# Three of six k-tile pairs of the last down projection by seven block products, and its last bank in two parts

## The chip, the cores and the metric

The kernel runs on one core of a Trainium2 chip. A core has a matrix engine (TensorE, PE in the profile; PEld is its weight load), a vector engine (VectorE, DVE), a scalar engine (ScalarE, ACT), a general engine (GpSimd, POOL) and a queue engine (SyncE, SP) that here only issues transfers. The metric is the device time in microseconds (us) of one execution; less is better.

## The reference

The reference is one block of a diffusion transformer: modulated normalisation, a projection, a gated recurrence and windowed attention side by side, a merge, and a feed-forward part with a depthwise convolution. The change lies in the last product of the feed-forward part alone.

```python
def conv_ffn(h, w_up, conv_w, conv_b, w_down):
    a, u = jnp.split(h @ w_up, 2, axis=-1)
    return (jax.nn.silu(depthwise_conv(a, conv_w, conv_b)) * u) @ w_down
...
        ffn_x = conv_ffn(modulate(x_mid, norm2_g[l], mod_x[:, 3], mod_x[:, 4]), w_up[l], conv_w[l], conv_b[l], w_down[l])
        new_x = x_mid + mod_x[:, 5][:, None, :] * ffn_x
```

There are 256 tokens and 2048 columns; the inner width is 5632, which is 44 tiles of 128 rows of `w_down` (k-tiles). All is in 32-bit floats.

## The kernel before

**Numbers in two parts.** TensorE works on a rounded 32-bit format here, so each operand is split into a high part and a low rest: ScalarE casts the raw tile to `whi`, and VectorE subtracts it from the raw tile to give `wlo` (`chunk`, lines 149 and 150, or `split`, lines 159 and 160). A product then takes three matmuls, high by high, high by low and low by high (`mm3`, line 72). Weights come from the array `wst` in the order of use, in tiles of 128 x 1024 (512 KB) into five raw buffers, by SP's queue; `whi` and `wlo` have three buffers each.

**The feed-forward part.** The 44 inner tiles are made in three groups of 16, 16 and 12 (`FF_GROUPS`). `up(g, gt)` makes a group: for each tile `duo` runs 16 steps of four matmuls into two banks, and `up_evac` folds these, applies the convolution and the gate, and splits the result into `gt`. After two groups, `down_two` adds up the first 32 k-tiles of the down projection; then the third group is made, and `down` adds up the last 12 k-tiles, multiplies by the gate (`gate`), adds to the rows kept in `xn`, and writes `out`. The down projection has 256 tokens (two halves of 128, the matmul's stationary side) by 2048 columns, which are taken as two halves of 1024 (`n`), each of two blocks of 512 (`c`). So a k-tile gives four products of 128 x 128 by 128 x 512 in each half, into four banks.

**Seven products.** `half` (lines 968 to 1030), used by `down_two` alone, takes k-tiles in pairs, so that the two token halves by the two tiles form a 2 x 2 block matrix, and the two tiles by the two column blocks another. For the pairs in `SEVEN`, the eight block products are replaced by seven, in the Winograd form of Strassen's rule. It needs sums of activation blocks, made once in `seven_acts` when the up tiles are evacuated, and sums of weight blocks, made in each half by VectorE from the raw tiles (`four`, lines 1011 to 1014) and then cast and split like any weight (`r2`, `r4`). Three products go straight into the `norm` banks of the plain pairs, and four into banks of their own (`sev`). After the last of the seven pairs VectorE joins the `sev` banks into `y` (lines 1023 to 1027), which is added to the `norm` banks at the end (line 1030). PSUM has eight banks: five in the pool `mm` (`bankm` in the profile) and three in `ms` (`banks`).

**The last down projection before.** `down` (lines 1053 to 1071) uses plain products: 12 k-tiles in each half, the last two taken bank by bank, so that the four banks close one after the other. For each bank VectorE multiplies by the gate (line 1067) and adds to `xn` (line 1068), and SP issues the output (line 1071).

**What sets the order.** A planner places the instructions: each engine's queue is fixed beforehand, by priority among those that the planner thinks ready. Program order is the priority. `tc.high_priority(offset)` moves work ahead: weight chunks by up to `LEAD` = 60 instructions, ends of a stage by `RUSH` = 120, and work at `-LAG` is put back by 60. Within `chunk`, `issue_after` keeps the casts and the splits in the order of the stream. Small tasks (`tasks`) are taken one at each `tick`, of which `duo` has four per up tile. SP's queue holds the loads and the outputs, and an issue waits there for its buffer with all others behind it.

Of the kernel before, what the change touches and what calls it, by code (L numbers as in the profile page):

```python
# [33 lines left out]
          ("m64", T)]  # L34
FF_GROUPS = [(0, 16), (16, 16), (32, 12)]
SEVEN = (1, 3, 5, 7, 9, 11, 13)


def offsets(fields):
# [12 lines left out]
def block_kernel(ctx, tc, xct, prm, cst, ada2, wst, out):  # L52
# [105 lines left out]
    def split(hi, lo, src):  # L158
        S.copy(hi, src)
        V.tensor_tensor(lo, src, hi.bitcast(F32), op=ALU.subtract)  # L160

    def exp_silu(dst, src, tmp):
        S.activation(tmp, src, AF.Exp, scale=-1.0)
# [761 lines left out]
    def up_evac(g, gt, i, oa, ou, fold=fold):  # L925
        f = FF_GROUPS[g][0] + i
        t, s = fs1[:, f % 4, :], fs2[:, f % 4, :]
        fold(s, oa)
        S.activation(t, s, AF.Identity, bias=cb[:, f:f + 1], scale=cw[:, f, 1:2])  # L929
        V.scalar_tensor_tensor(t[:, 1:T], s[:, 0:T - 1], cw[:, f, 0:1], t[:, 1:T], op0=ALU.mult, op1=ALU.add)  # L930
        V.scalar_tensor_tensor(t[:, 0:T - 1], s[:, 1:T], cw[:, f, 2:3], t[:, 0:T - 1], op0=ALU.mult, op1=ALU.add)
        fold(s, ou)
        S.activation(t, t, AF.Silu)
        V.tensor_tensor(s, s, t, op=ALU.mult)
# [13 lines left out]
    def seven_acts(p, gt, i, s1, s2):  # L948
        if not sums:
            sums["b"] = big.tile([P, 2, 2, 3 * P], F32R, name="sb", tag="sb")  # L950
        n = SEVEN.index(p)
        if n == 2:
            sums["a"] = big.tile([P, 5, 2, 3 * P], F32R, name="sa", tag="qo")
        d = sums["b"][:, n] if n < 2 else sums["a"][:, n - 2]
        sums[p] = d
        w = scr.tile([P, 512], F32, name="t")
        V.tensor_tensor(w[:, 0:P], s1[:, P:], s2[:, P:], op=ALU.subtract)
# [7 lines left out]
        for i in range(i0, FF_GROUPS[g][1]):  # L965
            up_evac(g, gt, i, *duo((h2, h2)))

    def half(g0, g1, norm, sev, y, own):
# [5 lines left out]
        def add(b, a, w, start=False, stop=False):  # L974
            mm3(b, *a, *w, start, stop)
        first = SEVEN[0]
        for p in range(16):
            k1, k2 = 2 * p, 2 * p + 1
            rb, (w21, w22) = chunk(2, fetch)
            a11, a21, a12, a22 = act(k1, 0), act(k1, 1), act(k2, 0), act(k2, 1)  # L980
            if p not in SEVEN:
                st0, sp = p == 0, p == 15
                if sp:
                    ra, (w11, w12) = chunk(2, fetch)
                    for b, u1, u2, v1, v2 in ((0, a11, a12, w11, w21), (1, a11, a12, w12, w22), (2, a21, a22, w11, w21),
                                              (3, a21, a22, w12, w22)):
                        add(norm[b], u1, v1)
                        add(norm[b], u2, v2, stop=True)
                    break
                add(norm[0], a12, w21, st0)  # L990
                add(norm[2], a22, w21, st0)
                add(norm[1], a12, w22, st0)
                add(norm[3], a22, w22, st0)
                ra, (w11, w12) = chunk(2, fetch)
                add(norm[0], a11, w11)
                add(norm[2], a21, w11)
                add(norm[1], a11, w12)
                add(norm[3], a21, w12)
                continue
            f, l = p == first, p == SEVEN[-1]  # L1000
            d = sums[p]
            s1, s2, s4 = [(d[:, 0, i * P:i * P + P], d[:, 1, i * P:i * P + P]) for i in range(3)]
            add(norm[0], a12, w21)
            add(norm[1], s4, w22)
            ra, (w11,) = chunk(1, fetch, home=own)
            add(sev[0], a11, w11, f, l)

            r4 = strm.tile([P, 1024], F32, name="araw", bufs=2)

            def four(raw):  # L1010
                V.tensor_tensor(raw[:, 0:512], ra[:, 0:512], ra[:, 512:], op=ALU.add)
                V.tensor_tensor(raw[:, 512:], ra[:, 512:], rb[:, 512:], op=ALU.add)  # L1012
                V.tensor_tensor(r4[:, 0:512], raw[:, 0:512], rb[:, 512:], op=ALU.add)
                V.tensor_tensor(r4[:, 512:], r4[:, 0:512], rb[:, 0:512], op=ALU.add)
            r2, (t1, t3) = chunk(2, four, "araw")
            add(sev[1], s1, t1, f, l)
            add(sev[3], a21, t3, f, l)

            _, (t2, t4) = chunk(2, lambda raw: None, r4)
            add(sev[2], s2, t2, f, l)  # L1020
            add(norm[2], a22, t4)
            if l:
                S.copy(y[0], sev[0])
                V.tensor_tensor(y[2], sev[2], y[0], op=ALU.subtract)
                V.tensor_tensor(y[1], sev[1], y[2], op=ALU.add)
                V.tensor_tensor(y[2], sev[3], y[2], op=ALU.add)
                V.tensor_tensor(y[3], sev[3], y[1], op=ALU.add)
        with tc.high_priority(offset=RUSH):
            for b in range(4):
                V.tensor_tensor(y[b], norm[b], y[b], op=ALU.subtract if b == 2 else ALU.add)  # L1030

    def down_two(g0, g1):
        own = big.tile([P, 2, 512], F32R, name="wone", tag="acc")
        own = [own[:, i] for i in range(2)]
# [4 lines left out]
        half(g0, g1, norm, sev, y0, own)  # L1039
# [4 lines left out]
        half(g0, g1, norm, sev, y1, own)  # L1044
        return y0, y1

    def gated(n, b, y):
        c = slice(512 * (b % 2), 512 * (b % 2) + 512)
        r = xn[:, b // 2, n, c]
        V.tensor_tensor(y, y, gate[n][:, c], op=ALU.mult)  # L1050
        V.tensor_tensor(r, r, y, op=ALU.add)

    def down(gt, nk):
        for n in range(2):
            norm = [bank() for _ in range(4)] if not n else [bank()] + [bank(ms) for _ in range(3)]
            w = {}
            for k in range(nk):
                ra, w[k] = chunk(2, fetch)
                ks = (k,) if k < nk - 2 else () if k < nk - 1 else (k - 1, k)
                for c, tt in ((0, 0), (0, 1), (1, 0), (1, 1)):  # L1060
                    for q in ks:
                        ts = slice(tt * P, tt * P + P)
                        mm3(norm[2 * c + tt], gt[:, q, 1, ts], gt[:, q, 0, ts], *w[q][c], q == 0, q == nk - 1)
            for c, tt in ((0, 0), (0, 1), (1, 0), (1, 1)):
                cs = slice(512 * c, 512 * c + 512)
                m = scr.tile([P, 512], F32, name="t")
                V.tensor_tensor(m, norm[2 * c + tt], gate[n][:, cs], op=ALU.mult)
                V.tensor_tensor(xn[:, tt, n, cs], xn[:, tt, n, cs], m, op=ALU.add)
                if n or tt:
                    o = slice(tt, tt + 1) if n else slice(0, 2)  # L1070
                    nc.sync.dma_start(out[:, o, n, cs], xn[:, o, n, cs])

    for i in range(2):
        up_evac(0, g0, i, os[2 * i], os[2 * i + 1], fold_pre)
# [30 lines left out]
    tasks += [lambda b=b: gated(0, b, y0[b]) for b in range(4)]  # L1105
    fs1 = big.tile([P, 4, T], F32, name="fs1", tag="kT")
    fs2 = big.tile([P, 4, T], F32, name="fs2", tag="va")
    up(2, g0)
    down(g0, FF_GROUPS[2][1])


_INS = ["xct", "prm", "cst", "ada2", "wst"]
# [147 lines left out]
```

## Time and profile before

| what | us |
|---|---|
| median of three runs (1665.59 to 1666.55) | 1665.6 |
| the profiled execution | 1666.65 |
| its span, first to last instruction | 1664.9 |
| TensorE busy in the span | 1648.2 |
| DVE busy in the span | 1241.8 |
| ACT busy in the span | 838.2 |

The span is the time between the first and the last instruction that the profile holds; what the execution has beyond it (1.75 us) lies around it. Busy time of TensorE is pipelined: matmuls overlap, and their ends are modelled, so the distance between starts is the better measure of their cost.

### The profile page before, as it was taken

Reading aid. Unit: us, or ns where it says so; the run is one execution under the profiler, and the core shown is the slowest. Engines: PE = TensorE matmul, PEld = TensorE weight load, DVE = VectorE, ACT = ScalarE, POOL = GpSimd, SP = SyncE. Lnnn points to the kernel's source line nnn. Section 1 sums busy time; section 2 is a strip of 40 time slices with the busy share of each in tenths; the row PEclk is TensorE's granted clock in tenths of the full one; section 3 lists DMA queues with packets and bytes.
Section 4 is the critical chain, followed back from the end, with each engine's and each line's share of the span. In section 5 each row is a group of like instructions: output and inputs, shape, how many; then the busy total and the mean of one; then the engine's idle time right before and its main releaser. Section 6 shows DMA issues by size and latency. Waiting matters only on the chain.

```text
span 1664.9 us, 23855 instructions
## 1 busy us (share of the span) xinstructions
PE 1648.2 (99%) x8981; PEld 1369.6 (82%) x8981; DVE 1241.8 (75%) x1914; ACT 838.2 (50%) x1267; POOL 68.1 (4%) x132
## 2 busy tenths in 40 slices
PE   8999999999999999999999999999999999999998
PEld 4668888888888888888888988888888888888887
DVE  3448986666879876768769887788776888986655
ACT  4336543444645654444445665555555555545542
POOL 0000100000000000001100000000000000000000
PEclk9999999999999999999999999999999999999999
DMA  9996834534466666977856567577555665655554
GB/s 379 407 372 233 301 114 156 189 114 152 165 214 210 223 213 227 335 238 277 286 203 232 186 216 266 200 278 263 192 180 187 202 214 197 222 196 190 187 189 148
DMA packets 104723, 372.83 MB, mean 224 GB/s; under 512 B 11536, under 2 KB 13728, under 8 KB 104608
## 3 DMA queue, kind: packets, MB, share of 16 engines
q1 hardware_dynamic: 86176, 304.20, 51.8%
q0 software_dynamic: 18432, 67.12, 12.4%
q8 instruction: 70, 1.15, 0.3%
q14 instruction: 45, 0.37, 0.1%
HBM read 369.16 MB, written 2.11 MB: 223 GB/s over the span
## 4 chain that ended last, share of the span: by engine, by line
PE 89%; DVE 4%; issue 3%; DMA 2%; ACT 1%; POOL 0%; SPq 0%; DVEq 0%; ACTq 0%; POOLq 0%
PE bankm L70 78%; PE banks L70 9%; DVE wlo L116 1%; DMA ringv<-in_wst_dram 1%; DMA ringkT<-in_wst_dram 1%; DVE acc L407 1%; PE banks L782 0%; PE banks L415 0%; DMA araw<-in_ada_dram 0%; DMA ringq<-in_wst_dram 0%; PE banks L615 0%; PE banks L810 0%; PE banks L607 0%; DMA xraw<-in_xct_dram 0%; PE banks L1080 0%
## 5 line engine op out<-in xcount | busy, mean ns | idle before, releaser
L116 DVE TENSOR_TENSOR wlo<-raw,whi 128x1024 fp32r<-128x1024 f32 (+2 forms) x410 | 499.0, 1218 | 228.7 <-ACT whi L115 225.5
L115 ACT CAST whi<-raw 128x1024 fp32r<-128x1024 f32 (+2 forms) x410 | 428.3, 1045 | 459.0 <-PE bankm L70 411.7
L70 PE MATMUL bankm<-hl,whi 128*128 128x512 f32 (+1 forms) x2048 | 627.7, 389 | 0.1
L70 PE MATMUL bankm<-whi,hl 128*128 128x512 f32 x1640 | 526.4, 393 | 1.0 <-ACT hl L252 0.9
L70 PE MATMUL bankm<-hl,wlo 128*128 128x256 f32 (+2 forms) x1760 | 396.6, 293 | 1.5 <-DVE wlo L116 1.5
L70 PEld LDWEIGHTS bankm<-hl,wlo 128*128 128x128 f32 x1760 | 330.8, 188 | 75.6 <-DVE wlo L116 2.4
L70 PEld LDWEIGHTS bankm<-whi,hl 128*128 128x128 f32 x1640 | 307.4, 188 | 66.1 <-ACT hl L252 2.6
L70 PEld LDWEIGHTS bankm<-hl,whi 128*128 128x128 f32 x2048 | 327.8, 189 | 17.8 <-DVE fs L916 0.4
L70 PE MATMUL bankm<-wlo,hl 128*128 128x512 f32 x820 | 320.3, 391 | 0.0
L70 PEld LDWEIGHTS bankm<-wlo,hl 128*128 128x128 f32 x820 | 154.1, 188 | 31.2 <-DVE wlo L116 0.2
L407 DVE SCALAR_TENSOR_TENSOR acc<-araw,csil,acc 128x1024 f32<-128x1024 f32 x120 | 153.5, 1279 | 2.1 <-DMA araw<-in_ada_dram 1.7
L150 DVE TENSOR_TENSOR wlo<-raw,whi 128x1024 fp32r<-128x1024 f32 x74 | 90.2, 1224 | 41.2 <-ACT whi L149 38.9
L402 POOL DMA_DIRECT2D araw<-in_ada_dram x128 | 67.9, 531 | 1091.4 <-DVE acc L407 569.3
L149 ACT CAST whi<-raw 128x1024 fp32r<-128x1024 f32 x74 | 77.7, 1053 | 66.4 <-PE bankm L70 41.1
L70 PE MATMUL bankm<-yb,whi 128*128 128x512 f32 x256 | 80.9, 397 | 0.0
L70 PEld LDWEIGHTS bankm<-yb,wlo 128*128 128x128 f32 x256 | 48.1, 188 | 11.2
L929 ACT ACTIVATE fs<-fs,prm 128x256 f32<-128x256 f32 x44 | 26.4, 601 | 52.0 <-DVE fs L464 52.0
L70 PE MATMUL bankm<-yb,wlo 128*128 128x256 f32 x256 | 50.6, 279 | 0.0
L149 ACT CAST whi<-araw 128x1024 fp32r<-128x1024 f32 x28 | 29.4, 1052 | 39.0 <-DVE araw L1012 34.9
L70 PE MATMUL banks<-whi,hl 128*128 128x512 f32 x136 | 46.3, 389 | 0.0
L70 PE MATMUL bankm<-whi,g 128*128 128x512 f32 x124 | 41.3, 390 | 0.0
L70 PEld LDWEIGHTS bankm<-yb,whi 128*128 128x128 f32 x256 | 39.2, 189 | 0.1
(291 smaller groups left out, 1523.3 us busy)
## 6 DMA issues: line engine op xcount, KB each, us to landing
raw<-in_wst_dram SPq DMA_DIRECT2D x489, 512.0 KB, 4.1
araw<-in_ada_dram POOLq DMA_DIRECT2D x128, 512.0 KB, 4.7
ringv<-in_wst_dram SPq DMA_DIRECT2D x24, 512.0 KB, 10.0
ringq<-in_wst_dram SPq DMA_DIRECT2D x20, 512.0 KB, 9.9
araw<-in_wst_dram SPq DMA_DIRECT2D x10, 512.0 KB, 9.9
xraw<-in_xct_dram SPq DMA_DIRECT2D x8, 512.0 KB, 6.9
raw<-in_wst_dram SPq DMA_DIRECT2D x7, 384.0 KB, 9.9
ringkT<-in_wst_dram SPq DMA_DIRECT2D x5, 512.0 KB, 9.9
```

The source lines that it names most:

```text
L70: return PE.matmul(o, l, r, start=start, stop=stop, skip_group_check=True)
L115: S.copy(hi, raw)
L116: self.last = V.tensor_tensor(lo, raw, hi.bitcast(F32), op=ALU.subtract)
L149: a = S.copy(hi[:, w], raw[:, w])
L150: b = V.tensor_tensor(lo[:, w], raw[:, w], hi[:, w].bitcast(F32), op=ALU.subtract)
L402: nc.gpsimd.dma_start(raw, ada2[idx])
L407: V.scalar_tensor_tensor(acc, raw, csil[:, kt, 0:1], acc, op0=ALU.mult, op1=ALU.add)
L929: S.activation(t, s, AF.Identity, bias=cb[:, f:f + 1], scale=cw[:, f, 1:2])
```

## The change

A second tuple, `LATE`, names pairs 17, 19 and 20 of the whole down projection, which are pairs 1, 3 and 4 of the six pairs of the last 12 k-tiles. `up_evac` and `seven_acts` make the activation sums for them too, in homes that are free by then. `half` becomes general and is used by `down` as well; the order of the two tiles of a pair in the weight stream is swapped accordingly.

For the first half (`n` = 0) the sums of weights are made on the spot, as in `down_two`. For the second half, three tasks (`make`) run during the up tiles of the third group: each loads the two raw tiles of its pair, makes the four sums on VectorE and splits them into `pm` or `pq`; `half` then takes them from `made`. The raw tiles of these pairs are loaded again in the second half, for the products that need no sums.

In the first half the joined `y` is added to the banks, then multiplied by the gate and added to `xn` (`gated`, put back by `LAG`), then written. In the second half `combine` calls `post` after the join: it multiplies each `y` by the gate and adds it to `xn`; at the end each `norm` bank is multiplied by the gate into `y`, added to `xn` and written. The last bank (`tail`) is summed, multiplied, added and written in two parts of 256 columns.

```diff
+LATE = (17, 19, 20)
...
+    def combine(sev, y, post):
+        S.copy(y[0], sev[0])
+        V.tensor_tensor(y[2], sev[2], y[0], op=ALU.subtract)
+        V.tensor_tensor(y[1], sev[1], y[2], op=ALU.add)
+        V.tensor_tensor(y[2], sev[3], y[2], op=ALU.add)
+        V.tensor_tensor(y[3], sev[3], y[1], op=ALU.add)
+        if post:
+            for b in range(4):
+                post(b)
...
+                        for w in [slice(0, 512)] if not tail or b < 3 else [slice(0, 256), slice(256, 512)]:
+                            add(norm[b][:, w], u1, [v[:, w] for v in v1])
+                            add(norm[b][:, w], u2, [v[:, w] for v in v2], stop=True)
...
+            s1, s2, s4, *s3 = sums[p]
+            add(norm[0], a12, w21, st0)
+            add(norm[1], s4, w22, st0)
+            ra, (w11,) = chunk(1, fetch, home=own)
+            add(sev[0], a11, w11, f, l)
+            if p in made:
+                t1, t3, t2, t4 = made[p]
+                add(sev[1], s1, t1, f, l)
+                add(sev[3], s3[0] if s3 else a21, t3, f, l)
+                add(sev[2], s2, t2, f, l)
+                add(norm[2], a22, t4, st0)
+                if l:
+                    combine(sev, y, post)
+                continue
...
-        if g < 2 and f // 2 in SEVEN:
+        if f // 2 in SEVEN + LATE:
...
+            if not n:
+                half(act, 6, seven, sums_of, (norm, lambda: sev), y, own)
+                with tc.high_priority(offset=-LAG):
+                    for b in (0, 2, 1, 3):
+                        gated(0, b, y[b])
+                        if b > 1:
+                            cs = slice(512 * (b % 2), 512 * (b % 2) + 512)
+                            nc.sync.dma_start(out[:, :, 0, cs], xn[:, :, 0, cs])
+                continue
+            half(act, 6, seven, sums_of, (norm, lambda: sev), y, own, made, lambda b: gated(1, b, y[b], ALU.subtract if b == 2 else ALU.add), True)
+            with tc.high_priority(offset=RUSH):
+                for b in range(4):
+                    tt, c = b // 2, b % 2
+                    for w in [slice(0, 512)] if b < 3 else [slice(0, 256), slice(256, 512)]:
+                        cs = slice(512 * c + w.start, 512 * c + w.stop)
+                        V.tensor_tensor(y[b][:, w], norm[b][:, w], gate[1][:, cs], op=ALU.mult)
+                        V.tensor_tensor(xn[:, tt, 1, cs], xn[:, tt, 1, cs], y[b][:, w], op=ALU.add)
+                        nc.sync.dma_start(out[:, tt, 1, cs], xn[:, tt, 1, cs])
...
+    def make(p, home):
+        rb, ra = [strm.tile([P, 1024], F32, name="raw", bufs=5) for _ in range(2)]
+        for i, r in enumerate((rb, ra)):
+            nc.sync.dma_start(r, wst[wst.shape[0] - 12 + 2 * p + i])
+        r2, r4 = [strm.tile([P, 1024], F32, name="araw", bufs=2) for _ in range(2)]
+        V.tensor_tensor(r2[:, 0:512], ra[:, 0:512], ra[:, 512:], op=ALU.add)
+        V.tensor_tensor(r2[:, 512:], ra[:, 512:], rb[:, 512:], op=ALU.add)
+        V.tensor_tensor(r4[:, 0:512], r2[:, 0:512], rb[:, 512:], op=ALU.add)
+        V.tensor_tensor(r4[:, 512:], r4[:, 0:512], rb[:, 0:512], op=ALU.add)
+        for i, r in enumerate((r2, r4)):
+            split(home[:, i, 0], home[:, i, 1], r)
+        made[p] = [(home[:, i, 0, c:c + 512], home[:, i, 1, c:c + 512]) for i in range(2) for c in (0, 512)]
+    for p, home in zip((1, 3, 4), (pm[:, 0], pm[:, 1], pq)):
+        tasks += [lambda: None] * 9 + [lambda p=p, home=home: make(p, home)]
     up(2, g0)
-    down(g0, FF_GROUPS[2][1])
+    assert not tasks
+    down(g0, made)
```

More of the change, by code (lines that the diff above doesn't have):

```diff
@@ L160, in split, with half, add, four @@
         V.tensor_tensor(lo, src, hi.bitcast(F32), op=ALU.subtract)
+    def combine(sev, y, post):
[7 more added lines that the diff above has]
+                post(b)
+    def half(act, n, seven, sums, banks, y, own, made={}, post=None, tail=False):
+        norm, sev = banks
+        def add(b, a, w, start=False, stop=False):
+            mm3(b, *a, *w, start, stop)
+        for p in range(n):
+            k1, k2 = 2 * p, 2 * p + 1
+            rb, (w21, w22) = chunk(2, fetch)
+            a11, a21, a12, a22 = act(k1, 0), act(k1, 1), act(k2, 0), act(k2, 1)
+            st0 = p == 0
+            plain = p == min(set(range(n)) - set(seven))
+            if p not in seven:
+                if p == n - 1:
+                    ra, (w11, w12) = chunk(2, fetch)
+                    for b, u1, u2, v1, v2 in ((0, a11, a12, w11, w21), (1, a11, a12, w12, w22), (2, a21, a22, w11, w21),
+                                              (3, a21, a22, w12, w22)):
+                        for w in [slice(0, 512)] if not tail or b < 3 else [slice(0, 256), slice(256, 512)]:
+                            add(norm[b][:, w], u1, [v[:, w] for v in v1])
+                            add(norm[b][:, w], u2, [v[:, w] for v in v2], stop=True)
+                    break
+                add(norm[0], a12, w21, st0)
+                add(norm[2], a22, w21, st0)
+                add(norm[1], a12, w22, st0)
+                add(norm[3], a22, w22, plain)
+                ra, (w11, w12) = chunk(2, fetch)
+                add(norm[0], a11, w11)
+                add(norm[2], a21, w11)
+                add(norm[1], a11, w12)
+                add(norm[3], a21, w12)
+                continue
+            f, l = p == seven[0], p == seven[-1]
+            if f:
+                sev = sev()
+            s1, s2, s4, *s3 = sums[p]
+            add(norm[0], a12, w21, st0)
+            add(norm[1], s4, w22, st0)
[10 more added lines that the diff above has]
+                continue
+            r4 = strm.tile([P, 1024], F32, name="araw", bufs=2)
+            def four(raw):
+                V.tensor_tensor(raw[:, 0:512], ra[:, 0:512], ra[:, 512:], op=ALU.add)
+                V.tensor_tensor(raw[:, 512:], ra[:, 512:], rb[:, 512:], op=ALU.add)
+                V.tensor_tensor(r4[:, 0:512], raw[:, 0:512], rb[:, 512:], op=ALU.add)
+                V.tensor_tensor(r4[:, 512:], r4[:, 0:512], rb[:, 0:512], op=ALU.add)
+            r2, (t1, t3) = chunk(2, four, "araw")
+            add(sev[1], s1, t1, f, l)
+            add(sev[3], s3[0] if s3 else a21, t3, f, l)
+            _, (t2, t4) = chunk(2, lambda raw: None, r4)
+            add(sev[2], s2, t2, f, l)
+            add(norm[2], a22, t4, st0)
+            if l:
+                combine(sev, y, post)
+        if post:
+            return
+        with tc.high_priority(offset=RUSH):
+            for b in range(4):
+                V.tensor_tensor(y[b], norm[b], y[b], op=ALU.subtract if b == 2 else ALU.add)
@@ L162, in exp_silu, with parts_of @@
+    def parts_of(hi, lo):
+        return [(hi[:, i:i + P], lo[:, i:i + P]) for i in range(0, hi.shape[-1], P)]
     def exp_silu(dst, src, tmp):
@@ L950, in seven_acts @@
             sums["b"] = big.tile([P, 2, 2, 3 * P], F32R, name="sb", tag="sb")
[L951 removed]
+        n = (SEVEN + LATE).index(p)
         if n == 2:
             sums["a"] = big.tile([P, 5, 2, 3 * P], F32R, name="sa", tag="qo")
[L954 removed]
+        d = sums["b"][:, n % 7] if n % 7 < 2 else spare2 if n > 7 else sums["a"][:, n - 2]
         sums[p] = d
@@ L966, in up, with down_two @@
             up_evac(g, gt, i, *duo((h2, h2)))
-    def half(g0, g1, norm, sev, y, own):
+    def down_two(g0, g1):
+        own = big.tile([P, 2, 512], F32R, name="wone", tag="acc")
+        own = [own[:, i] for i in range(2)]
         def act(k, tt):
@@ L972, in act @@
             return gt[:, k % 16, 1, ts], gt[:, k % 16, 0, ts]
[L974 to L1034, printed above, removed]
+        sums_of = {p: parts_of(sums[p][:, 0], sums[p][:, 1]) for p in SEVEN}
         sev = [bank()]
@@ L1038, in down_two @@
         y0 = [scr.tile([P, 512], F32, name="t") for _ in range(3)] + [scr.tile([P, 512], F32, name="rs", bufs=1)]
-        half(g0, g1, norm, sev, y0, own)
+        half(act, 16, SEVEN, sums_of, (norm, lambda: sev), y0, own)
         norm = [bank()] + [bank(ms) for _ in range(3)]
@@ L1043, in down_two, with gated @@
         y1 = [y1[b // 2][:, b % 2] for b in range(4)]
-        half(g0, g1, norm, sev, y1, own)
+        half(act, 16, SEVEN, sums_of, (norm, lambda: sev), y1, own)
         return y0, y1
-    def gated(n, b, y):
+    def gated(n, b, y, op=ALU.add):
         c = slice(512 * (b % 2), 512 * (b % 2) + 512)
@@ L1050, in gated @@
         V.tensor_tensor(y, y, gate[n][:, c], op=ALU.mult)
-        V.tensor_tensor(r, r, y, op=ALU.add)
-    def down(gt, nk):
-        for n in range(2):
[L1055 to L1071, printed above, removed]
@@ new lines, in gated, with down, act @@
+        V.tensor_tensor(r, r, y, op=op)
+    def down(gt, made):
+        def act(k, tt):
+            ts = slice(tt * P, tt * P + P)
+            return gt[:, k, 1, ts], gt[:, k, 0, ts]
+        sums_of = {p - 16: parts_of(sums[p][:, 0], sums[p][:, 1]) for p in LATE}
+        seven = tuple(sums_of)
+        own = [own2[:, i] for i in range(2)]
+        for n in range(2):
+            if n:
+                norm = [bank()] + [bank(ms) for _ in range(3)]
+                sev = [bank() for _ in range(4)]
+                y = [big.tile([P, 2, 512], F32, name="y" + t, tag=t) for t in ("kT", "va")]
+                y = [y[b // 2][:, b % 2] for b in range(4)]
+            else:
+                sev = [bank()]
+                norm = [bank() for _ in range(4)]
+                sev += [bank(ms) for _ in range(3)]
+                y = [scr.tile([P, 512], F32, name="t") for _ in range(3)] + [scr.tile([P, 512], F32, name="rs", bufs=1)]
+            if not n:
[6 more added lines that the diff above has]
+                            nc.sync.dma_start(out[:, :, 0, cs], xn[:, :, 0, cs])
+                continue
+            half(act, 6, seven, sums_of, (norm, lambda: sev), y, own, made, lambda b: gated(1, b, y[b], ALU.subtract if b == 2 else ALU.add), True)
+            with tc.high_priority(offset=RUSH):
+                for b in range(4):
+                    tt, c = b // 2, b % 2
[4 more added lines that the diff above has]
+                        nc.sync.dma_start(out[:, tt, 1, cs], xn[:, tt, 1, cs])
```

9 lines of the change are left out of this document (8 added, 1 removed).

## The prediction

> **What bounds the kernel now.** I read four views in this order: the page's busy shares, the table of stretches, the timeline of VectorE and of TensorE around the last down projection, and the DMA issues. First the page, then the table of stretches (first half of the big down projection, the last 12 up tiles, the last down projection up to its last matmul; the columns are the busy time of each engine, the granted clock and the DMA).
>
> ```profile
> span 1664.9 us, 23855 instructions
> PE 1648.2 (99%) x8981; PEld 1369.6 (82%) x8981; DVE 1241.8 (75%) x1914; ACT 838.2 (50%) x1267; POOL 68.1 (4%) x132
> ...
> core 0: us, PE busy (x) PEld busy (x) DVE busy (x) ACT busy (x) POOL busy (x), PEclk, DMA share, GB/s
> 1297.00:1379.20 82.20, 81.95 (x360) 66.91 (x359) 73.41 (x88) 45.06 (x50) 0.00 (x0) 1.00 0.62 205
> ...
> 1461.00:1594.40 133.40, 133.40 (x768) 116.48 (x767) 92.87 (x128) 69.87 (x104) 0.00 (x0) 1.00 0.55 190
> 1594.40:1660.00 65.60, 65.60 (x290) 53.89 (x288) 37.84 (x42) 24.92 (x27) 0.00 (x0) 1.00 0.50 167
> ```
>
> TensorE is busy 99% at the full clock (1.00 in each stretch), and in the last two stretches it never pauses: 133.40 of 133.40 and 65.60 of 65.60 us. DVE has room: 92.87 of 133.4 us in the up tiles, 37.84 of 65.6 in the last down projection. In the big down projection, which already uses the seven-product pairs, DVE stands at 73.41 of 82.2 in the half where it makes the weight sums.
>
> The end is told by three timelines: TensorE's first and last matmul of the last down projection, two pieces of the chain of waits, and DVE's last eight operations (start, length, engine, line).
>
> ```profile
> 1594.44 0.40 PE L70 MATMUL bankm<-whi,hl 128*128 128x512 f32 x1
> 1659.62 0.39 PE L70 MATMUL banks<-whi,hl 128*128 128x512 f32 x1
> ```
> ```profile
> 1628.05 2.04 PE banks L70 x9
> 1630.09 0.68 PE bankm L70 x3
> ```
> ```profile
> 1655.97 0.69 DVE L1067 TENSOR_TENSOR t<-bankm,cst 128x512 f32<-128x512 f32 x1 [1.77 <-PE bankm L70]
> 1656.69 0.69 DVE L1068 TENSOR_TENSOR xn<-xn,t 128x512 f32<-128x512 f32 x1
> 1657.33 0.69 DVE L1067 TENSOR_TENSOR t<-banks,cst 128x512 f32<-128x512 f32 x1
> ...
> 1660.05 0.69 DVE L1067 TENSOR_TENSOR t<-banks,cst 128x512 f32<-128x512 f32 x1
> 1660.77 0.69 DVE L1068 TENSOR_TENSOR xn<-xn,t 128x512 f32<-128x512 f32 x1
> ```
>
> One matmul of 512 columns costs (2.04 + 0.68) / 12 = **0.2267 us** of TensorE's time; its 0.39 us is length, overlapped with the next. There are 12 tiles x 2 halves x 4 products x 3 = 288 of them. 287 x 0.2267 = 65.06 us after 1594.44 is 1659.50, and the row says 1659.62, so only 0.12 us was lost. DVE follows at 1.36 us per bank (1655.97 to 1657.33), exactly the pace of TensorE (6 x 0.2267), so one bank's two operations stick out: DVE ends at 1660.77 + 0.69 = 1661.46, and the output's landing and the end marker take the 3.44 us to 1664.9.
>
> **The change part by part.**
>
> Products. Three pairs of six lose one of eight products in each half: 3 x 2 x 3 = 18 matmuls, 18 x 0.2267 = 4.08 us of TensorE. The two-part end puts 12 matmuls of 256 columns for 6 of 512, some tenths more; it matters only where TensorE sets the end, which the next part denies.
>
> Behind the products. The seven-product form ends with sums. After the last seven pair DVE runs four operations to join the `sev` banks, and in the second half `post` adds eight more (multiply by the gate and add to `xn`, for four banks), all of 512 columns. The join's first operation reads `sev[2]`, the last of the four `sev` banks to close, and everything else follows from it; even the gate product of `y[0]` has to wait until the join has read `y[0]`. Then each `norm` bank takes its multiply and add, which overwrite `y[b]` and so stand behind `post(b)`. That makes 12 + 6 operations of 512 columns and 4 of 256 on DVE after `sev[2]`. The seven pairs are 1, 3 and 4 of 0 to 5, so behind `sev[2]` TensorE has just 3 + 24 matmuls: 27 x 0.2267 = 6.1 us. The pace of such operations, from the gates after the big down projection, and of 256-column ones from the up tiles:
>
> ```profile
> 1463.76 0.68 DVE L1050 TENSOR_TENSOR ykT<-ykT,cst 128x512 f32<-128x512 f32 x1
> 1464.37 0.68 DVE L1050 TENSOR_TENSOR yva<-yva,cst 128x512 f32<-128x512 f32 x1
> ...
> 1585.54 0.42 DVE L464 TENSOR_TENSOR fs<-bankm,fs 128x256 f32<-128x256 f32 x1
> 1589.22 0.43 DVE L934 TENSOR_TENSOR fs<-fs,fs 128x256 f32<-128x256 f32 x1
> ```
>
> Independent ones start 0.61 us apart, one that needs its predecessor 0.72 (1655.97 to 1656.69). The 12: 12 x 0.61 = 7.3 at least, 12 x 0.665 = 8.0 if every second waits; I take the middle, 7.6. The three full banks: 3 x 1.36 = 4.1. The four halves at 0.42 to 0.43: 1.6. Together **13.3 us** (13.7 with 8.0, and 12.6 if no operation on a full bank waits either: 7.3 + 6 x 0.61 + 1.6), twice the 6.1 us of matmuls beside it. So the end moves from TensorE to DVE, and the removed products of the last pair are worth nothing there.
>
> Where `sev[2]` closes. Up to it TensorE runs 288 - 18 - 27 = 243 matmuls. Without a stall the last one starts at 1594.44 + 242 x 0.2267 = 1649.30 and ends at 1649.69. Two stalls come on top, both in the first half, where DVE makes the weight sums on the spot. The big down projection shows the work of one seven pair and one plain pair on DVE, with TensorE's use of the first sums:
>
> ```profile
> 1316.42 2.58 DVE L150 TENSOR_TENSOR wlo<-raw,whi 128x1024 fp32r<-128x1024 f32 x2 [0.59 <-ACT whi L149]
> 1318.92 0.68 DVE L150 TENSOR_TENSOR wone<-raw,wone 128x512 fp32r<-128x512 f32 x1
> ...
> 1321.45 0.69 DVE L1014 TENSOR_TENSOR araw<-araw,raw 128x512 f32<-128x512 f32 x1
> 1322.06 2.50 DVE L150 TENSOR_TENSOR wlo<-araw,whi 128x1024 fp32r<-128x1024 f32 x2
> 1324.62 1.23 DVE L150 TENSOR_TENSOR wlo<-raw,whi 128x1024 fp32r<-128x1024 f32 x1
> ```
> ```profile
> 1324.20 0.39 PE L70 MATMUL banks<-wlo,sa 128*128 128x512 f32 x1
> ```
>
> A seven pair takes DVE 1.25 (its first tile, half of the 2.50 from 1316.42 to 1318.92) + 5.70 (1318.92 to 1324.62) = 6.95 us, where TensorE needs 21 x 0.2267 = 4.76. A plain pair takes the other 1.25 and 1.2 for the tile at 1324.62, 2.45 against 24 x 0.2267 = 5.44. Alternating, 9.4 stands against 10.2 and DVE keeps up; the low part of the first sums was ready at 1322.06 + 1.23 = 1323.29 and wanted at 1324.20 (the first matmul with `wlo` in the banks of the small pool), a margin of 0.91 us. Pairs 3 and 4 of the new order are both seven pairs. Between their first sums DVE needs 6.95, TensorE 4.76: short by 2.19, less the margin is **1.3 us** of stall. Pair 5, the last, uses both its tiles at once. DVE makes the low part of the second sums, of tile one and of tile two after that, 3 x 1.2 = 3.6 us, and TensorE has 12 matmuls = 2.72 until it wants the last of these: **0.9 us**. (Slots don't help: three `whi`/`wlo` buffers hold one and a half pairs.) In the second half the sums are ready beforehand, so a seven pair costs DVE only 1.85 us, and nothing stalls.
>
> The other stall is at the start. The first seven pair meets the evacuation of the last up tile on DVE and in the banks, as it did in the big projection, where TensorE's starts lie too far apart:
>
> ```profile
> 1301.76 0.39 PE L70 MATMUL bankm<-whi,sb 128*128 128x512 f32 x1
> 1302.19 0.50 PE L70 MATMUL banks<-whi,sb 128*128 128x512 f32 x1
> 1302.53 0.40 PE L70 MATMUL banks<-whi,hl 128*128 128x512 f32 x1
> 1303.14 0.50 PE L70 MATMUL banks<-whi,sb 128*128 128x512 f32 x1 [0.21 <-ACT whi L149]
> 1303.47 0.40 PE L70 MATMUL bankm<-whi,hl 128*128 128x512 f32 x1
> ```
>
> Four starts with 0.43, 0.34, 0.61 and 0.33 us before the next instead of 0.23 are 0.8 us lost. The bank count is the same (one `sev`, four `norm`, all five of `mm`), so I take **0.7** over the 0.12 lost now, with 0 and 1.5 as bounds. The sum of the stalls is 0.8 + 1.3 + 0.9 = 3.0 (0 if the planner's order and buffers cover all, 5 if the join's operations also slip between the tiles of pair 5).
>
> Work moved into the up tiles. Three times DVE makes the sums of weights: four operations of 0.68 and two splits of 1.22 = 5.2 us, with two loads of 512 KB on SP's queue and two raw slots of five; the activation sums come on top, of whose operations these are two rows:
>
> ```profile
> L957 DVE TENSOR_TENSOR t<-fs x7: 284/286/293, 989.3 to 1256.7; 128x128 f32<-128x128 f32 x7
> L160 DVE TENSOR_TENSOR sa<-t,sa 128x384 fp32r<-128x384 f32 x3 | 1.7, 555 | 0.4 <-ACT sa L159 0.4
> ```
>
> Four of 0.286 and a split of 0.555 after one of about 0.28, less 0.14 for the shorter split of the even tile, give 1.8. In all 3 x (5.2 + 1.8) = 21 us, so DVE goes from 92.87 to 114 of 133.4 us, 85%. The big projection ran at 73.41 of 82.2 (89%) with a loss of 0.25 us, so I cost it at **0.2 us**; the cover is DVE's idle 3.4 us per up tile ((133.4 - 92.87) / 12) and the three buffered tiles. Without cover each block of 5.2 overruns one tile's idle by 1.8, 5.4 us in all. Behind a make's two loads on SP the stream's loads queue, and ScalarE's casts wait for these; the stretch moves 190 GB/s at a DMA share of 0.55, and 6 loads of 512 KB in 133.4 us add 24 GB/s, so I add nothing. In the first half's end the two outputs wait on SP for `gated` as they did for the old multiply and add, and the second half's loads queue behind them; there were as many DVE operations before them as now less the join, and DVE has 30 us there for some 21 us of work, so this too is 0 (2 if a load came late by one output's wait).
>
> The last output. Its size falls from 256 to 128 KB.
>
> ```profile
> out_dram<-xn SPq DMA_DIRECT2D x2, 512.0 KB, 4.2
> out_dram<-xn SPq DMA_DIRECT2D x4, 256.0 KB, 2.0
> ```
>
> By these rows, 4.2 us for 512 KB and 2.0 for 256, proportion would give 1.0 less; if the time doesn't shrink, 0. I take the middle, 0.5. The Trainium skill ("DMA: Bandwidth & Descriptors", section "Anatomy of one DMA") speaks against proportion: a transfer on GpSimd's path has a fixed part of about 2 us, mostly the receipt of the write, and only the rest goes with the bytes. By that rule the gain would be 0.3 (an estimate, 128 KB at the page's 436 GB/s) and the sum 0.2 higher; the rows, on SP's path, do not bear the fixed part out, since half the bytes took half the time, though the larger two ran beside the stream.
>
> The sum. `sev[2]` closes at 1649.69 + 3.0 + 0.2 = 1652.9; 0.05 for the signal and 13.3 later DVE ends at 1666.2. Before it was 1661.46: +4.8, less 0.5 for the output is **+4.3 us**. Against the profiled execution's own 1666.65 (its span and 1.75 around it) that is 1670.9; the median of the three runs lies 1.05 lower at 1665.6, so I predict **1669.9 us**.
>
> **The rivals.**
>
> A, no stall in the first half at pairs 3 to 5. For it: the planner may let DVE run ahead during the plain pairs, and 0.59 us of idle per period stood there. Against: that idle was a wait on a buffer, not on work. The stalls of 1.3 and 0.9 go: 1667.7.
>
> B, the up tiles stall too. For it: 21 us more on DVE and two of five raw slots lent out. Against: the 89% above. At half of the 5.4 it gives 1672.6.
>
> C, the other side, not slower: TensorE still sets the end. The mechanism is that the planner pulls the products of pair 4 in the second half ahead, since their sums are made early and wait for no streamed tile, so that the join and `post` run beside the matmuls. For it: TensorE is 99% busy and DVE is not. It decides once `sev[2]` closes 4.3 us, 19 matmuls, before where I put it (then as before), and at 6 us earlier TensorE sets the end alone: 1665.6 - 4.08 = 1661.5 without stalls, 1664.5 with all 3.0. Against: the join starts from `sev[0]`, which needs pair 4's streamed second tile. The Trainium skill ("Perfetto Trace Analysis", section "Identifying the Most-Contended Engine") would have it so: the engine with the highest occupancy is the one to optimise first. The page of the profile bears that out for the whole span, at 99%; whether it holds for the last 15 us is what this rival asks.
>
> D, the two-part end does not do what it says. It shortens the wait behind the last bank only if DVE is waiting for that bank. With DVE 7 us behind, the four short operations cost 1.6 us for 1.36; this 0.2 is in the forecast, and C is the only case where the split helps.
>
> **How the numbers follow.** Forecast 0.51, A 0.24, B 0.17, C 0.08; D is no case of its own. A measurement of this kernel tells about 0.2%, 3.3 us, from no change: below 1662.3 is faster, above 1668.9 slower. The forecast's own range is 1668 to 1672 (chain 12.6 to 13.7, stalls 2 to 4), nine tenths of it above the line: 0.46. With B 0.17 and 0.04 of A that makes 0.67 slower. C is faster only where the stalls stay away too, 0.04. The rest, 0.05 of the forecast, 0.20 of A and 0.04 of C, is 0.29 for the same. The range reaches from A with the shortest chain and the quickest output, 1667.7 - 0.7 - 0.5 = 1666.5, and a little of C, 1665.8, to a little beyond B, 1673.0.
>
> **What would show it.** Right: in the second half DVE runs some 22 operations without a gap after the last read of `sev[2]`, TensorE's last matmul ends about 7 us before DVE's last operation, and the chain of waits ends in DVE for 13 us, not 5.5. TensorE shows pauses of about 1 us in pair 4 and at pair 5 of the first half and none in the second; the up stretch stays at 133.4 to 133.6 us. Wrong: TensorE's last matmul within 2 us of DVE's end (C), an up stretch longer by over 1 us (B), or a first half of 135 x 0.2267 = 30.6 us without pauses (A).

## The result and the profile after

The changed kernel takes 1669.53 us (median of 15 runs, 1667.71 to 1670.41) against 1665.59 us before (median of 15, 1664.64 to 1666.57): 3.9 us more, a ratio of 1.0020 with a 95% interval of 1.0014 to 1.0027. The forecast was 1669.9.

The page of the changed kernel, and its row of the table of stretches for the 12 up tiles; behind it the row of the kernel before, cut at the same two matmuls. The columns are the stretch and its length, then the busy time of PE, PEld, DVE, ACT and POOL, the granted clock and the DMA.

```profile
span 1666.2 us, 23950 instructions
PE 1645.8 (99%) x8969; PEld 1365.7 (82%) x8969; DVE 1280.9 (77%) x1990; ACT 849.9 (51%) x1287; POOL 68.1 (4%) x132
...
1458.94:1592.69 133.75, 133.75 (x770) 116.71 (x768) 110.09 (x165) 77.76 (x116) 0.00 (x0) 1.00 0.62 213
```
```profile
1460.69:1594.44 133.75, 133.75 (x770) 116.79 (x768) 93.11 (x129) 70.18 (x104) 0.00 (x0) 1.00 0.55 190
```

TensorE is busy for 2.4 us less in all (the rest of the 4.08 us of removed matmuls is taken by short pauses, most of which busy time counts as work), and VectorE for 39 us more. The up tiles take 133.75 us in both kernels, with VectorE at 110.09 in place of 93.11: the sums made there cost no time.

The last down projection begins at 1592.69 us. These rows are TensorE's first and last matmul in it.

```profile
1592.69 0.40 PE L71 MATMUL bankm<-whi,hl 128*128 128x512 f32 x1
...
1656.84 0.28 PE L71 MATMUL banks<-whi,hl 128*128 128x256 f32 x1
```

And this is VectorE behind `sev[2]` in the second half (line 165 reads it; 165 to 168 are the join, 1076 and 1077 the gate operations of `post`, 1112 and 1113 those of the `norm` banks):

```profile
1651.04 0.69 DVE L165 TENSOR_TENSOR yva<-bankm,ykT 128x512 f32<-128x512 f32 x1 [2.90 <-PE bankm L71]
1651.77 0.69 DVE L166 TENSOR_TENSOR ykT<-bankm,yva 128x512 f32<-128x512 f32 x1
1652.38 0.68 DVE L1076 TENSOR_TENSOR ykT<-ykT,cst 128x512 f32<-128x512 f32 x1
...
1657.17 0.69 DVE L1112 TENSOR_TENSOR ykT<-banks,cst 128x512 f32<-128x512 f32 x1
1657.77 0.69 DVE L1076 TENSOR_TENSOR yva<-yva,cst 128x512 f32<-128x512 f32 x1
...
1661.97 0.76 DVE L1112 TENSOR_TENSOR yva<-banks,cst 128x256 f32<-128x256 f32 x2
1662.64 0.76 DVE L1113 TENSOR_TENSOR xn<-xn,yva 128x256 f32<-128x256 f32 x2
```

TensorE is done at 1656.84 + 0.28 = 1657.12. VectorE works without a gap of over 0.03 us from 1651.04 to 1662.64 + 0.76 = 1663.40, 22 operations in 12.36 us, of which the last 6.28 us stand alone. Before, 1.46 us stood alone.

TensorE's pauses lie in the first half. Below are its rows at pair 1 and at pairs 4 and 5; starts of neighbours should be 0.23 us apart.

```profile
1599.53 0.39 PE L71 MATMUL bankm<-whi,sb 128*128 128x512 f32 x1
1599.96 0.50 PE L71 MATMUL banks<-whi,sb 128*128 128x512 f32 x1
1600.30 0.40 PE L71 MATMUL banks<-whi,hl 128*128 128x512 f32 x1
1600.90 0.50 PE L71 MATMUL banks<-whi,sb 128*128 128x512 f32 x1 [0.21 <-ACT whi L150]
...
1616.43 0.73 PE L71 MATMUL banks<-whi,hl 128*128 128x512 f32 x2
1617.73 0.50 PE L71 MATMUL banks<-wlo,hl 128*128 128x512 f32 x1 [0.57 <-DVE wlo L151]
...
1620.07 1.30 PE L71 MATMUL bankm<-whi,hl 128*128 128x512 f32 x5
1621.60 0.50 PE L71 MATMUL bankm<-whi,hl 128*128 128x512 f32 x1 [0.23 <-ACT whi L150]
```

The profile names what ended the wait at each: a cast of ScalarE at pair 1, VectorE's low part (`wlo`) in pair 4, and a cast again at pair 5. Summed over all starts that are late by over 0.08 us, pair 1 loses 1.0 us, pair 4 1.3, pair 5 0.5.

For all runs below I use one measure from their profiled executions: the time from the first matmul of the last down projection to TensorE's last, to VectorE's last, and to the end of the span. The ends are taken from the traces to 0.01 us; the page rounds the span to 0.1.

| kernel | first matmul at | TensorE's last | VectorE's last | span's end | pauses in the first half |
|---|---|---|---|---|---|
| before | 1594.44 | 65.57 | 67.03 | 70.42 | 0.1 |
| changed | 1592.69 | 64.43 | 70.71 | 73.55 | 2.8 |
| e1_h1_two | 1595.26 | 65.13 | 67.19 | 70.03 | 2.8 |
| e2_h0_two | 1593.07 | 63.23 | 69.51 | 72.35 | 1.0 |
| e3_fewer_ops | 1593.24 | 64.43 | 68.61 | 71.31 | 2.8 |
| e4_one_piece | 1592.67 | 64.36 | 70.70 | 73.71 | 2.8 |
| e5_mix | 1593.15 | 63.71 | 66.02 | 68.85 | 1.0 |
| e7_mix_one | 1593.62 | 63.24 | 65.61 | 68.60 | 1.0 |
| e6_banks | 1594.33 | 62.43 | 64.63 | 67.46 | 0.3 |
| e8_banks_both | 1592.39 | 62.46 | 64.77 | 67.61 | 0.3 |

In the profiled pair the stage costs 73.55 - 70.42 = 3.13 us more; the runs say 3.9, with an interval of 2.3 to 4.5. The first column shows why the times of two single executions can't be set against each other, but their stages can: in the first nine rows the stage starts anywhere in a range of 2.6 us, though the work up to there is the same but for the sums in the up tiles.

### The profile page after: what moved, and what is told of

It is laid out like the page before. It is cut to its first block, busy times and chain, and to the rows that moved or that the text cites. A ratio compares the mean times of both kernels' runs of the same rounds, so it can differ in the third digit from the quotient of the medians.

```text
span 1666.2 us, 23950 instructions
## 1 busy us (share of the span) xinstructions
PE 1645.8 (99%) x8969; PEld 1365.7 (82%) x8969; DVE 1280.9 (77%) x1990; ACT 849.9 (51%) x1287; POOL 68.1 (4%) x132
## 4 chain that ended last, share of the span: by engine, by line
PE 87%; DVE 6%; issue 3%; DMA 2%; ACT 1%; POOL 0%; SPq 0%; DVEq 0%; ACTq 0%; POOLq 0%
PE bankm L71 76%; PE banks L71 8%; DVE wlo L117 1%; DVE acc L492 1%; DMA ringv<-in_wst_dram 1%; DMA ringkT<-in_wst_dram 1%; PE banks L867 0%; PE banks L500 0%; DVE wlo L151 0%; DMA ringq<-in_wst_dram 0%; PE banks L700 0%; PE banks L895 0%; DMA araw<-in_ada_dram 0%; ACT whi L150 0%; PE banks L692 0%
## 5 line engine op out<-in xcount | busy, mean ns | idle before, releaser
L71 PE MATMUL bankm<-whi,hl 128*128 128x512 f32 x1600 | 514.3, 393 | 1.2 <-ACT hl L337 0.9
L71 PEld LDWEIGHTS bankm<-whi,hl 128*128 128x128 f32 x1600 | 299.7, 188 | 65.4 <-ACT hl L337 2.6
L71 PE MATMUL bankm<-wlo,hl 128*128 128x512 f32 x800 | 312.3, 391 | 0.0
L71 PEld LDWEIGHTS bankm<-wlo,hl 128*128 128x128 f32 x800 | 150.3, 188 | 30.5 <-DVE wlo L117 0.2
L151 DVE TENSOR_TENSOR wlo<-raw,whi 128x1024 fp32r<-128x1024 f32 x68 | 82.7, 1223 | 18.4 <-ACT whi L150 15.8
L150 ACT CAST whi<-raw 128x1024 fp32r<-128x1024 f32 x68 | 71.4, 1054 | 45.8 <-PE bankm L71 22.6
L150 ACT CAST whi<-araw 128x1024 fp32r<-128x1024 f32 x34 | 35.6, 1052 | 45.0 <-DVE araw L226 40.3
L151 DVE TENSOR_TENSOR wlo<-araw,whi 128x1024 fp32r<-128x1024 f32 x34 | 41.4, 1222 | 2.2 <-ACT whi L150 1.3
```

The source lines that it names most:

```text
L71: return PE.matmul(o, l, r, start=start, stop=stop, skip_group_check=True)
L150: a = S.copy(hi[:, w], raw[:, w])
L151: b = V.tensor_tensor(lo[:, w], raw[:, w], hi[:, w].bitcast(F32), op=ALU.subtract)
```

## The experiments

**Is it the operations behind `sev[2]`? Two runs.** The theory is that VectorE's chain behind the last `sev` bank sets the end; the rival is that TensorE's pauses do, and the end only follows. The first run takes pair 4 out of the seven-product pairs in the second half, so that `sev[2]` closes a pair earlier.

```diff
-            half(act, 6, seven, sums_of, (norm, lambda: sev), y, own, made, lambda ...
+            half(act, 6, seven[:2], sums_of, (norm, lambda: sev), y, own, made, lambda ...
```

> The second half takes only pairs 1 and 3 by seven products; pair 4 is taken by plain products (with the activation block that was stored as a difference for the seven products, so that block's share of the output is changed). Theory (the operations on VectorE behind sev[2] set the end): three matmuls more, 0.7 us, but sev[2] closes 24 matmuls earlier and the join and the eight gate operations lie beside TensorE; VectorE ends within 2 us of TensorE instead of 6.3, in all 4.3 us less than the changed kernel, about 1665.3 us. Rival (the loss sits in TensorE's pauses in the first half, the end is only a shift of it): 0.7 us more than the changed kernel, about 1670.2.

Measured: 1666.22 us, 3.3 less than the changed kernel (ratio to the kernel before 1.0003, 0.9994 to 1.0012); the stage is 3.52 shorter.

```profile
1660.11 0.28 PE L71 MATMUL banks<-whi,hl 128*128 128x256 f32 x1
```
```profile
1648.86 0.69 DVE L165 TENSOR_TENSOR yva<-bankm,ykT 128x512 f32<-128x512 f32 x1 [0.48 <-PE bankm L71]
1649.59 0.69 DVE L166 TENSOR_TENSOR ykT<-bankm,yva 128x512 f32<-128x512 f32 x1
...
1661.70 0.75 DVE L1113 TENSOR_TENSOR xn<-xn,yva 128x256 f32<-128x256 f32 x2
```

VectorE ends 2.06 us behind TensorE (1662.45 against 1660.39) in place of 6.28, though TensorE has 0.7 us more to do and its pauses are the same 2.8. That is the theory's sign and most of its size; the 0.8 that is missing I put down to a split of a streamed tile (1653.28 to 1654.42), which lies between the gate operations: VectorE has hardly a gap from 1649.59 on there too. No run takes that split away.

The second run leaves TensorE's work alone and takes three operations off VectorE's chain, 19 in place of 22 (five of 512 columns fewer, two of 256 more): `post` does nothing, and each bank is added to `y`, multiplied and added to `xn` when it closes.

```diff
-            half(..., made, lambda b: gated(1, b, y[b], ...), True)
+            half(..., made, lambda b: None, True)
...
+                        V.tensor_tensor(y[b][:, w], norm[b][:, w], y[b][:, w], op=ALU.subtract if b == 2 else ALU.add)
-                        V.tensor_tensor(y[b][:, w], norm[b][:, w], gate[1][:, cs], op=ALU.mult)
+                        V.tensor_tensor(y[b][:, w], y[b][:, w], gate[1][:, cs], op=ALU.mult)
```

> Same products in the same order; in the second half the eight gate operations of post are left out, and each bank is added to y, multiplied by the gate and added to xn once it closes: 4 + 9 operations of 512 columns and 6 of 256 behind sev[2] in place of 18 and 4. The output is the reference's. Theory (their number on VectorE sets the end): 2.5 for the join, 9 x 0.62 and 6 x 0.36 are 10.3 us in place of 12.4, 2.1 us less, about 1667.4; TensorE's end stays. Rival (the end is set by something else, such as the output's transfer): no change, 1669.5; or longer, 1670, since three operations a bank are slower than TensorE's 1.36 us.

Measured: 1666.99 us, 2.5 less (ratio 1.0008, 0.9999 to 1.0017); the stage is 2.24 shorter, TensorE's last matmul stands at 64.43 as in the changed kernel, and the chain takes 1661.85 - 1651.59 = 10.26 us.

```profile
1651.59 0.69 DVE L165 TENSOR_TENSOR yva<-bankm,ykT 128x512 f32<-128x512 f32 x1 [2.90 <-PE bankm L71]
...
1661.43 0.42 DVE L1114 TENSOR_TENSOR xn<-xn,yva 128x256 f32<-128x256 f32 x1
```

With TensorE's times unchanged to 0.01 us, the end follows VectorE's operations: that is shown. The rival falls as the sole cause; the pauses still count through the moment at which `sev[2]` closes, as the next run shows.

**Do neighbouring seven pairs make the pauses?** In the first half pair 4 becomes plain.

```diff
-                half(act, 6, seven, sums_of, (norm, lambda: sev), y, own)
+                half(act, 6, seven[:2], sums_of, (norm, lambda: sev), y, own)
```

> The first half takes only pairs 1 and 3 by seven products, pair 4 by plain ones (with the stored difference block, so that share of the output is changed); the second half is that of the changed kernel. Theory (two neighbouring seven pairs are more than VectorE can feed): the pauses of 1.3 us in pair 4 and 0.5 us at pair 5 go, three matmuls come back (0.7), 1.1 us less than the changed kernel, about 1668.4; the pause of 1.0 us at pair 1 stays. Rival (the pauses come from the planner's order or the loads, not from neighbours): they stay and it is 0.7 us longer, about 1670.2.

Measured: 1667.50 us, 2.0 less (ratio 1.0012, 1.0003 to 1.0021); the stage is 1.20 shorter, as expected to 0.1. Only pair 1's pause of 1.0 us is left; behind it no start in the stage is late by over 0.08 us.

**Does the two-part end bring anything?** Once in the changed kernel, once in the kernel of the next paragraph.

```diff
-            half(..., made, lambda b: gated(1, b, y[b], ...), True)
+            half(..., made, lambda b: gated(1, b, y[b], ...), False)
...
-                    for w in [slice(0, 512)] if b < 3 else [slice(0, 256), slice(256, 512)]:
+                    for w in [slice(0, 512)]:
```

> The changed kernel with the last bank summed, multiplied, added and written in one piece of 512 columns. The output is the reference's. Theory (VectorE runs behind anyway, so the two parts shorten no wait): VectorE's last operation moves by 0.1 us or less, and only the larger last output counts, 3.4 us from VectorE's end to the span's end in place of 2.8: 0.5 us more, about 1670.0. Rival (the two parts overlap half a bank of TensorE's work with VectorE's): 0.7 us for that and 0.6 for the output, 1.3 more, about 1670.8.

Measured: 1668.69 us beside 1666.38 for the kernel before (ratio 1.0018, 1.0009 to 1.0027); the changed kernel's own ratio is 1.0020, so no difference shows. In the stage, VectorE's last operation stays (70.70 for 70.71) and the output's end takes 3.01 us in place of 2.84. So the two parts bring 0.2 us in the output alone. I had expected 0.6 there.

> The kernel with pairs 1 and 3 in the first half and 1, 2 and 3 in the second, with the last bank in one piece. The output is the reference's. There TensorE sets the end. Theory (the four short operations cost more than the overlap brings): VectorE ends 1.5 us behind TensorE in place of 2.3, TensorE 0.1 earlier, the output 0.6 later: 0.3 less than with two parts, about 1663.9. Rival (the two parts are worth half a bank once TensorE sets the end): 0.7 and 0.6 more, about 1665.5.

Measured: 1664.20 us beside 1666.38 (ratio 0.9989, 0.9980 to 0.9997), and for the same kernel with two parts 0.9992 (0.9983 to 1.0001): not told apart by time. The stage is 0.24 shorter, near the sum that was expected (0.3), but by another way. VectorE did not come within 1.5 us of TensorE: it ends 2.37 behind. It has no gap of over 0.04 us there either, so I was wrong that TensorE sets the end in this kernel.

**A version that avoids both losses.** The first half takes pairs 1 and 3, no neighbours; the second takes 1, 2 and 3, so that the join lies a pair earlier. Pair 2 is plain in one half and of seven products in the other, so its activation difference gets a home of its own.

```diff
-LATE = (17, 19, 20)
+LATE = (17, 18, 19)
...
+                half(act, 6, seven[::2], sums_of, (norm, lambda: sev), y, own)
...
+        own3 = n > 8
+        s3 = w[:, 3 * P:] if own3 else s1[:, P:]
+        V.tensor_tensor(s3, s1[:, P:], s1[:, 0:P], op=ALU.subtract)
...
-    for p, home in zip((1, 3, 4), (pm[:, 0], pm[:, 1], pq)):
+    for p, home in zip((1, 2, 3), (pm[:, 0], pm[:, 1], pq)):
```

> Pairs 1 and 3 by seven products in the first half (sums on the spot), pairs 1, 2 and 3 in the second (weight sums made during the up tiles; the activation difference of pair 2 is kept apart so that both forms can use it). The output is the reference's. Theory: 15 matmuls less (3.4 us), the pause of 1.0 at pair 1 stays, no neighbours on the spot, and the join lies a pair earlier, beside 51 matmuls; with the output's 0.6 less 3.0 us less than the kernel before, about 1662.6. Rival (VectorE's work in the last half is too much wherever it lies): no better than 1665.

Measured: 1664.24 us beside 1665.57 (ratio 0.9992, 0.9983 to 1.0001), 5.3 us less than the changed kernel; its stage is 1.57 shorter than that of the kernel before, not the 3.0 expected.

```profile
1645.68 0.68 DVE L165 TENSOR_TENSOR yva<-bankm,ykT 128x512 f32<-128x512 f32 x1
1646.40 0.69 DVE L166 TENSOR_TENSOR ykT<-bankm,yva 128x512 f32<-128x512 f32 x1
...
1650.00 1.22 DVE L151 TENSOR_TENSOR wlo<-raw,whi 128x1024 fp32r<-128x1024 f32 x1
1651.14 0.69 DVE L1081 TENSOR_TENSOR xn<-xn,ykT 128x512 f32<-128x512 f32 x1
...
1658.41 0.75 DVE L1117 TENSOR_TENSOR xn<-xn,yva 128x256 f32<-128x256 f32 x2
```
```profile
1651.28 0.50 PE L71 MATMUL bankm<-wlo,hl 128*128 128x512 f32 x1 [0.15 <-DVE wlo L151]
```

VectorE has no gap from 1645.68 to 1659.16: 13.5 us, in which a split of a streamed tile stands between the gate operations. A pair earlier is just enough to bring the end 2.3 us behind TensorE. TensorE's last matmul is 0.5 later than I had it, 0.4 of which is a pause in the second half, at 58.1 us of the stage. It is the matmul at 1651.28, which waits for that split: ScalarE's cast for it was done at 1649.27, but it stood behind seven operations of the join and the gate on VectorE. So the chain cost TensorE time there too.

**What makes the pause at pair 1?** The same kernel, but the banks are dealt out of both pools for both roles, so that the fourth `norm` sum of pair 0 need not wait for a bank of the last up tile.

```diff
-                sev = [bank()]
-                norm = [bank() for _ in range(4)]
-                sev += [bank(ms) for _ in range(3)]
+                norm = [bank(), bank(), bank(), bank(ms)]
+                sev = [bank(ms), bank(ms), bank(), bank()]
```

The banks of the second half are dealt out anew along with these.

> The kernel with pairs 1 and 3 in the first half and 1, 2 and 3 in the second, but in the first half three norm banks and two sev banks come from the pool of five and one norm bank and two sev banks from the pool of three, so that the plain pair 0 need not wait for the banks of the last up tile; the second half's banks follow. The output is the reference's. Theory (the pause of 1.0 us at pair 1 comes from the bank that the fourth norm sum waits for, which holds back weight buffers): 0.3 us or less remain, 0.8 less, about 1663.4. Rival (VectorE is late there with the last up tile's evacuation beside the weight sums): the pause stays at 0.8 or more, about 1664.2.

Measured: 1663.27 us beside 1666.38 (ratio 0.9983, 0.9974 to 0.9991); the stage is 1.38 shorter than in e5_mix, and 3.0 shorter than in the kernel before.

```profile
1600.46 0.39 PE L71 MATMUL bankm<-whi,sb 128*128 128x512 f32 x1
1600.69 0.39 PE L71 MATMUL bankm<-wlo,sb 128*128 128x512 f32 x1
1600.91 0.39 PE L71 MATMUL bankm<-whi,sb 128*128 128x512 f32 x1
1601.14 0.84 PE L71 MATMUL banks<-hl 128*128 128x512 f32 x3
1601.82 0.39 PE L71 MATMUL banks<-whi,sb 128*128 128x512 f32 x1
```

Pair 1 now runs through, 0.23 us from start to start, with the last up tile's evacuation still beside it on VectorE; 0.27 us of pauses are left in all. So it was the dealing of the banks, not VectorE's queue. The rows of e5_mix agree:

```profile
1597.79 0.42 DVE L549 TENSOR_TENSOR fs<-bankm,fs 128x256 f32<-128x256 f32 x1
1598.27 0.50 PE L71 MATMUL bankm<-whi,hl 128*128 128x512 f32 x1
...
1599.33 2.00 ACT L150 CAST whi<-araw 128x1024 fp32r<-128x1024 f32 x2 [0.48 <-PE bankm L71]
1600.40 2.36 DVE L151 TENSOR_TENSOR wlo<-araw,whi 128x1024 fp32r<-128x1024 f32 x2 [0.52 <-ACT whi L150]
```

The evacuation reads its bank until 1598.21, and the matmul due at 1598.14 starts at 1598.27. ScalarE's cast of the weight sums then waits for a matmul, and VectorE stands idle for 0.52 us in front of its low part. The new dealing also changes the order of evacuation, casts and splits on both engines, so the run shows what the banks and that order bring together. The gain is 0.6 more than expected; 0.4 of it is the pause in the second half of e5_mix, which is gone as well. That part is not shown to come from the banks: e7_mix_one, with the banks of e5_mix, has no such pause either.

The same exchange in the big down projection:

```diff
-        sev = [bank()]
-        norm = [bank() for _ in range(4)]
-        sev += [bank(ms) for _ in range(3)]
+        norm = [bank(), bank(), bank(), bank(ms)]
+        sev = [bank(ms), bank(ms), bank(), bank()]
         y0 = ...
```

> The kernel of the run before (pairs 1 and 3, then 1, 2 and 3; banks of both pools in both roles) with the same exchange of banks in the big down projection, whose first seven pair paused 0.8 us before any change. The output is the reference's. Theory (the bank of the fourth norm sum makes that pause): 0.6 less than the run before, about 2.8 to 3.6 us less than the kernel before, a ratio of 0.998. Rival (there the pause has another cause): the ratio and the pause stay, 0.9983 or more.

Measured: 1661.88 us beside 1665.59 (ratio 0.9980, 0.9971 to 0.9989). This is the fastest version here, 3.7 us less than the kernel before. The step over the run before lies within the intervals, so time alone does not show it; the trace does: late starts in the first 12 us of the big projection's first half sum to 1.0 us in e6_banks and 0.2 in e8_banks_both.

## Why the prediction was right

**The sum.** Forecast 4.3 us more, 1669.9; measured 3.9 more by the runs, 3.13 in the stage of the two profiled executions. Both lie in the forecast's range (1668 to 1672, 2.4 to 6.4 more), and its reason, VectorE's chain behind `sev[2]`, is shown by e1_h1_two and e3_fewer_ops. That the number came within 0.4 is in part luck: laid against the stage the terms are 1.2 too high in sum, and the median difference lies 0.8 above the stage's, which the interval allows and nothing here explains. The terms one by one:

- The chain, 13.3 us with 12.6 as its shortest: measured 12.36. This is the term that was mis-sized, by 0.9. I let an operation that needs its predecessor start 0.72 us after it in half of the cases. The planner put others between, so nearly all start 0.60 apart (1657.17 to 1657.77), and the four short ones 0.33 where I counted 0.4 (four at 0.42 to 0.43 are 1.7 besides, not 1.6).
- The pause at pair 1, 0.8: measured 1.0. I named the evacuation and the banks together; by e6_banks it goes with another dealing of the banks while the evacuation stays.
- The pauses at pair 4 (1.3) and pair 5 (0.9): measured 1.3 and 0.5. e2_h0_two removes both by parting the neighbours. At pair 5 I supposed that the tiles' low parts hold TensorE; the row names ScalarE's cast.
- The up tiles, 0.2: measured 0.00 (133.75 in both). VectorE's added work there was 17.0 us (110.09 less 93.11), where I counted 21.
- The last output, 0.5 less: VectorE's end to the span's end went from 3.39 to 2.84, 0.55 less. By e4_one_piece only 0.17 of it comes from the two parts; the rest is a shorter time behind the landing, of which the last section has the numbers. So the size of this term came out by chance. The rows of the outputs (second column of numbers: us to landing) show how little half the bytes save:

```profile
out_dram<-xn SPq DMA_DIRECT2D x3, 256.0 KB, 2.0
out_dram<-xn SPq DMA_DIRECT2D x2, 128.0 KB, 1.8
```

The middle between proportion (1.0) and nothing was taken for want of a row. 2.0 us for 256 KB and 1.8 for 128 agree with a large fixed part, as the Trainium skill ("DMA: Bandwidth & Descriptors", section "Anatomy of one DMA") has it for GpSimd's path, whose rule gave 0.3; its 2.0 us for the fixed part is above the whole 1.8 measured here on SP's path. I had read the two rows of before as against it, and the larger one had run beside the stream.

**The rivals.** A (no pause at pairs 3 to 5) falls by the rows at 1617.73 and 1621.60. B (the up tiles stall) falls by the 133.75 us. C (TensorE sets the end) falls with VectorE alone for the last 6.28 us; the rule of the Trainium skill that it went with ("Perfetto Trace Analysis", section "Identifying the Most-Contended Engine") agrees with the whole span, 99% busy (the weight loads, by which that section would judge TensorE's headroom, 82%, still above VectorE's 75%), and does not hold for this stage's end, where e3_fewer_ops shortened the stage without touching TensorE. D was right that the two parts shorten no wait; that they would cost 0.2 on VectorE was not so (70.71 against 70.70).

**What I had not seen.** In the big projection I took busy time, 81.95 of 82.2, for the loss. Matmuls overlap, so short pauses vanish in it: the starts show 1.0 us lost there. And a profiled pair is not the median: one load of GpSimd's queue, early in the kernel and the same in both, took 6.91 us in the execution before and 5.18 in the one after, as the chain of waits has it,

```profile
142.03 6.91 DMA araw<-in_ada_dram
```
```profile
141.99 5.18 DMA araw<-in_ada_dram
```

and everything from there on runs 1.75 us earlier after. So the spans differ by 1.3 us, the stages by 3.13 and the medians by 3.9.

## What to carry to other kernels

Counting products saved on the busiest engine does not give the time at the end: work out what still has to run behind the last input of the joining step, on whichever engine, and lay it against what is left to hide it. A scheme that keeps pace on average can fail where two of its heavy steps stand side by side, and the order of the steps is then worth as much as their number. When a stage starts with a pause, look which memory bank the first sums wait for before blaming an engine's queue.

## What the runs showed of the hardware

VectorE starts operations of 128 x 512 floats 0.60 us apart when neighbours are independent and 0.72 us apart when the second needs the first, though each lasts 0.69. Operations of 128 x 256 start 0.33 us apart. Shortening the last output from 256 to 128 KB took 0.2 us off its landing (2.0 to 1.8), but in the changed kernel its issue came 0.12 us behind VectorE's end, where it was 0.03 in e4_one_piece. With the same 256 KB as the last output, the kernel before needed 3.39 us from VectorE's end to the span's end and e4_one_piece 3.01. The difference is not in the output: its landing took 2.02 and 2.00 us, and the end of the span came 1.34 and 0.97 us behind it. Why, no run here shows.
